# A shorter root, a sink as a score column, and gate products on the tensor engine, in an fp32 decoder layer

## The chip, the cores and the metric

The kernel runs on one core of a Trainium2 chip. The metric is the device time of one execution in microseconds. A core has five engines with a queue of instructions each: PE (TensorE, matrix products; its weight loads are shown apart as PEld), DVE (VectorE), ACT (ScalarE), POOL (GpSimd) and SP (SyncE, which here issues nearly all DMAs). Each engine works through its queue in order, and waits for another on semaphores.

## The reference

One layer of a hybrid decoder (Hymba-style): a sequence of 512, width 1024, 8 heads of 64 in group A (sliding window of 128, with a sink for each head), 8 in group B (native sparse attention with the branches cmp, sel and win, each with a sigmoid gate). Cut to what matters:

```
mod = silu(c) @ w_ada + b_ada;  shift, scale, gate = split(mod, 3)
h = rms_norm(x, norm_gain) * (1 + scale) + shift
q_a, k_a, v_a, z_a, q_b, kc, vc, ks, vs, kw, vw, z_b, g_b = split(h @ w_in)
qk_norm(t, gain) = t * rsqrt(mean(t * t) + EPS) * gain            # on every q and k
# group A, sliding window with a sink:
m = max(max(logits), sink);  e = exp(logits - m)
p = e / (sum(e) + exp(sink - m));  o_a = p @ v
# group B: o_cmp (31 compressed blocks), o_sel, o_win
gb = sigmoid(g_b + b_nsa_gate)
o_b = gb[0] * o_cmp + gb[1] * o_sel + gb[2] * o_win
y = concat(o_a * silu(z_a), o_b * silu(z_b))
out = x + gate * (y @ w_out)
```

## The kernel before

Everything is fp32. A large product is made of three fast ones: the weight is split into an upper and a lower half (`split`: `wh` is a copy by ACT, `wl` the difference `raw - wh`), the activations likewise (`hh`, `hl`), and each block of 128 in the contraction takes `wh·hh`, `wl·hh` and `wh·hl`. A weight matrix comes in four pieces p. `wl` is DVE's work for p = 0, 1, 2 (`WL_DVE`), and POOL's for p = 3.

The stages, with their places in the profiled execution: the start (modulation with `c`, sum of squares, normalised `h`), then the first projection (q, k, v of group A), to about 62 us; stream 1, which projects the compressed, selected and window keys and values and the q of group B, woven with 16 "a" slots of attention, to about 165; stream 2, which makes the z projections, the compressed attention and the gate, woven with 28 "b" slots, to about 310; the output projection in eight units, each with a DMA of its result.

A slot is one head pair's block of 128 queries in one branch. It runs in four steps, one iteration apart: scores (PE into PSUM, a custom DVE instruction that adds the bias and keeps the running minimum `nm`, Exp on ACT with its sum in `dn`), scale (DVE: `rr = 1/dn`, times P), transposes (PE, copied by ACT), and value products (PE). `run` takes the slots in turn and advances the stream by a budget for each, 3.6 in stream 1 and 1.5 in stream 2; a generator in the stream yields the cost of what it has just issued. The work that follows a projection (`posts`: norms, q and k scaling, `cmp_mlp`, the gate) is woven into the following units by `with_posts`. A scheduler then orders the instructions by their dependences; only the start has its order written out (`in_order`).

`rsqrt` is the root of the norms, on DVE: an integer guess and three Newton steps, twelve operations on tiles of 128x1 to 128x40, in 11 calls. Four of these belong to the q of group B (128x8): `post_q` squares (`sq`, L510), sums (`ss_q`, L514), scales (L517), takes the root (L100 to L109, ending in `n_y`), multiplies (`qn`, L523), splits (`qc`, L526 and L527), and PE transposes `qc` (L532).

In an "a" slot the sink is a small chain of its own: `es = nm + sink` (L880), its Exp (L886), `dn += es` (L901). In a "b" slot `rr` is multiplied by the head's gate (`grev`, L905, and L895 with L898 in the slot that holds two branches of the first block).

`gate_slice(q)` makes a quarter of the output gate's modulation on POOL: eight products of a weight block with a column of silu(c) (`gt`, L707, and L704 for the first), and seven sums into `gacc` (L708). At the output stage PE sums `gacc` over the partitions (L1008). The weights come through `rawp`, a ring of five buffers that also carries all other weights; `load_next` issues the next DMA on SP's queue.

One tile `longs` holds `gacc`, the values `va`, `vs`, `vw`, `kg`, `gsig`, `grev`, the ones, `nsink` and columns for the modulation; another, `hhl`, holds the 16 halves of `h` and an identity. In the profile their parts read as `longs` and `hhl`.

Of the kernel before, what the change touches and what calls it, by code (L numbers as in the profile page):

```python
# [77 lines left out]
def hybrid_layer_kernel(ctx, tc, A, out):  # L78
# [11 lines left out]
    def T2(dt, name):  # L90
        return t2.tile([128, S], dt, name=name, tag="t2")

    def rsqrt(v, n):
# [8 lines left out]
        DVE.tensor_scalar(hv, v, -0.5, None, op0=OP.mult)
        cur = yi.bitcast(F32)
        DVE.tensor_tensor(p, hv, cur, op=OP.mult)
        for n in range(3):
            DVE.tensor_tensor(t, p, cur, op=OP.mult)
            DVE.scalar_tensor_tensor(y, t, 1.5, cur, op0=OP.add, op1=OP.mult)
            if n < 2:
                DVE.scalar_tensor_tensor(p, t, 1.5, p, op0=OP.add, op1=OP.mult)  # L109
# [14 lines left out]
    hhl = con.tile([128, 16 * S + 128], F32R, name="hhl")  # L124
    hh, hl = ([hhl[:, S * (8 * e + k):S * (8 * e + k + 1)] for k in range(8)] for e in range(2))
    ident_r = hhl[:, 16 * S:16 * S + 128]
    longs = con.tile([128, 3040], F32, name="longs")
    used = [0]

    def keep(*shape):  # L130
        n = int(np.prod(shape))
        used[0] += n
        t = longs[:, used[0] - n:used[0]]
        return t if len(shape) == 1 else t.rearrange("p (a b) -> p a b", a=shape[0])

    gacc = keep(D)
    va, vs, vw = (keep(NB, 128) for _ in range(3))
    kg = keep(4, HD)
    gsig, grev = keep(NB, 24), keep(NB, 24)
    ones, nsink, sc_col, prm1 = keep(1), keep(8), keep(8), keep(8)  # L140
# [25 lines left out]
    def split(g, p):  # L166

        if g in COL:
            src = raws[g, p % 2][:, :, 128 * (p // 2):128 * (p // 2) + 128]
# [6 lines left out]
        ACT.activation(wh, src, AF.Copy)  # L176
        (DVE if p in WL_DVE else POOL).tensor_tensor(wl, src, wh.bitcast(F32), op=OP.subtract)  # L177
# [405 lines left out]
    def cmp_x(kv, bank):  # L583

        tt = T2(F32, "cmpt").rearrange("p (g u) -> p g u", g=2)
        for g in range(2):
            for par in range(2):
                src = bank[64 * g:64 * g + 64, par:512:2]
                dst = tt[64 * par:64 * par + 64, g, :]
                if g:  # L590
# [65 lines left out]

    def cmp_attn():
        kTc = X["kTc"]
        L = [mp.tile([128, 2, 2, 128], F32, name="pa", bufs=3) for _ in range(2)]
        for g in range(2):  # L660
            ps = ps_s.tile([128, 512], F32, name="s")
            for r in range(4):
# [34 lines left out]
            yield 0.44  # L697

    def gate_slice(q):
        g = gacc[:, 256 * q:256 * q + 256]  # L700
        for j in range(8):
            a = raws[f"gate{q}", j // 4][:, j % 4]
            if j == 0:
                POOL.tensor_scalar(g, a, sc_col[:, 0:1], None, op0=OP.mult)  # L704
            else:
                t = mp.tile([128, 256], F32, name="gt", bufs=4)
                POOL.tensor_scalar(t, a, sc_col[:, j:j + 1], None, op0=OP.mult)  # L707
                POOL.tensor_tensor(g, g, t, op=OP.add)  # L708
# [146 lines left out]
    def slot_scores(sl):  # L855
        kind, r, br, i = sl["id"]
        lo = max(0, i - 1) * 128 if kind == "a" else 0
        w = (i + 1) * 128 - lo
# [7 lines left out]
        for g in range(2):  # L866
# [9 lines left out]
            DVE.tensor_tensor_reduce(out=P[:, g, 0:w], in0=ps, in1=bt, scale=1.0, scalar=init,  # L876
                                     op0=OP.add, op1=OP.min, accum_out=nm[:, g:g + 1])
        if kind == "a":
            es = sm.tile([128, 2], F32, name="es", bufs=4)
            DVE.tensor_tensor(es, nm, sinks[:, r:8:4], op=OP.add)  # L880
# [4 lines left out]
        if kind == "a":
            ACT.activation(es, es, AF.Exp)  # L886
        sl.update(P=P, dn=dn, w=w, lo=lo)

    def slot_scale(sl):
        kind, r, br, i = sl["id"]  # L890
        P, dn, w = sl["P"], sl["dn"], sl["w"]
        if br == 3:
            rr = sm.tile([128, 2, 2], F32, name="rr2", bufs=2)
            DVE.reciprocal(rr, dn)
# [4 lines left out]
            return
        if kind == "a":  # L900
            DVE.tensor_tensor(dn, dn, sl["es"], op=OP.add)  # L901
        rr = sm.tile([128, 2], F32, name="rr", bufs=4)
        DVE.reciprocal(rr, dn)
        if kind == "b":
            DVE.tensor_tensor(rr, rr, grev.rearrange("p i (g r c) -> p i g r c", g=2, c=3)[:, i, :, r, br], op=OP.mult)  # L905
        for g in range(2):
            if kind == 'a' and g: ACT.activation(P[:, g, 0:w], P[:, g, 0:w], AF.Copy, scale=rr[:, g:g + 1])
            else: DVE.tensor_scalar(P[:, g, 0:w], P[:, g, 0:w], rr[:, g:g + 1], None, op0=OP.mult)
# [175 lines left out]
```

## Time and profile before

| | |
|---|---|
| median of 3 runs | 356.04 us (355.6 to 356.32) |
| profiled execution | 355.26 us, of which span 353.5 us |
| mean granted PE clock | 0.989 |
| busy: PE, DVE, ACT, POOL | 331.8, 248.9, 198.7, 70.7 us |
| DMA | 44.28 MB, mean 125 GB/s |

A row of the profile names a line of the kernel, an engine, an operation, and the tiles written and read (`out<-in`). Windows give the busy time of each engine in a stretch; a group's row has its busy time, the mean ns of one, and the idle time ahead of it with what ended that. A wait reads `PE pt L532 <- DVE qc L527`: PE's instruction at L532 was idle until DVE's at L527 ended; then come the total, the times and the longest.

### The profile page before, as it was taken

To read this page: it belongs to the slowest core of one execution; us is meant where nothing else is said; L and a number is where in the kernel's file an instruction comes from. 1 tells how busy PE (TensorE), PEld (TensorE's weight loads), DVE (VectorE), ACT (ScalarE), POOL (GpSimd) and SP (SyncE) were. 2 spreads that over 40 slices of the span, in tenths; PEclk is the share of its full clock that TensorE was granted. 3 is DMA by queue.
4 is the path that set the end of the run, shared out by engine and by line. 5 is a ranking of instruction groups with operands and counts; after the bars stand their busy time and mean duration, and the time that the engine had idled before them with its cause. 6 is when DMAs were issued, how large, how long until landed. Compare 5 with 4: busy or idle time off the path is not lost.

```text
span 353.5 us, 6376 instructions
## 1 busy us (share of the span) xinstructions
PE 331.8 (94%) x2239; PEld 262.2 (74%) x2240; DVE 248.9 (70%) x823; ACT 198.7 (56%) x510; POOL 70.7 (20%) x81
## 2 busy tenths in 40 slices
PE   8999999999799998697898899999999999999995
PEld 4478888788766797686855586788788788788884
DVE  3657797999886689996957699878767673643321
ACT  6665538367476585574754667867777666322200
POOL 1000001020200017646449007700100100110110
PEclk9999999999899999998999999999999999999999
DMA  8999926700155442233173035201101203124221
GB/s 266 390 410 406 376 96 161 259 0 3 61 170 194 144 124 86 92 119 121 31 209 121 0 111 162 85 4 59 61 2 47 75 4 117 59 62 118 73 76 59
DMA packets 31063, 44.28 MB, mean 125 GB/s; under 512 B 1766, under 2 KB 23398, under 8 KB 31032
## 3 DMA queue, kind: packets, MB, share of 16 engines
q1 hardware_dynamic: 29880, 41.79, 35.3%
q10 hardware_dynamic: 1152, 2.10, 2.1%
q8 instruction: 17, 0.28, 0.3%
q14 instruction: 14, 0.11, 0.1%
HBM read 41.74 MB, written 2.14 MB: 124 GB/s over the span
## 4 chain that ended last, share of the span: by engine, by line
PE 66%; DVE 16%; POOL 5%; DMA 5%; ACT 3%; issue 2%; SPq 1%; DVEq 0%; ACTq 0%; POOLq 0%
PE pj L494 23%; PE po L944 7%; PE s L871 6%; PE sq L301 5%; PE pj L484 5%; PE pt L926 3%; DMA raw<-in_w_gate 3%; POOL gt L707 3%; PE skv L327 2%; PE pt L919 2%; PE skv L302 2%; PE s L609 2%; POOL longs L708 2%; DVE wl L177 2%; DVE pp L600 1%
## 5 line engine op out<-in xcount | busy, mean ns | idle before, releaser
L177 POOL TENSOR_TENSOR wl<-raw,wh 128x512 fp32r<-128x512 f32 (+1 forms) x13 | 18.8, 1447 | 253.0 <-PE pj L494 100.3
L484 PE MATMUL pj<-wh,hhl 128*128 128x256 f32 (+1 forms) x256 | 55.1, 298 | 0.0
L494 PE MATMUL pj<-hhl,wh 128*128 128x512 f32 x160 | 52.1, 405 | 0.0
L176 ACT ACTIVATE wh<-raw 128x512 fp32r<-128x512 f32 (+1 forms) x52 | 31.6, 626 | 26.3 <-PE pj L494 25.3
L484 PEld LDWEIGHTS pj<-wh,hhl 128*128 128x128 f32 x256 | 42.1, 192 | 2.3 <-issue 2.2
L484 PE MATMUL pj<-wl,hhl 128*128 128x256 f32 (+1 forms) x128 | 37.8, 295 | 1.9 <-DVE wl L177 1.9
L177 DVE TENSOR_TENSOR wl<-raw,wh 128x512 fp32r<-128x512 f32 (+1 forms) x39 | 26.9, 697 | 17.5 <-PE pj L494 14.3
L883 ACT ACTIVATE pp<-pp,nm 128x256 f32<-128x256 f32 (+2 forms) x48 | 29.3, 612 | 16.4 <-DVE nm L876 15.8
L494 PEld LDWEIGHTS pj<-hhl,wh 128*128 128x128 f32 x160 | 28.1, 188 | 8.0 <-issue 3.8
L944 PE MATMUL po<-ptT,longs 128*64 128x128 f32 x432 | 33.7, 284 | 0.0
L876 DVE CUSTOM_DVE_ANT_0 pp<-s,bias 128x256 f32<-128x256 f32 (+2 forms) x48 | 25.3, 552 | 10.0 <-PE s L871 6.3
L494 PE MATMUL pj<-hhl,wl 128*128 128x512 f32 x80 | 31.8, 398 | 0.0
L944 PEld LDWEIGHTS po<-ptT,longs 128*64 128x64 f32 x432 | 24.1, 138 | 9.7 <-issue 4.6
L707 POOL TENSOR_SCALAR gt<-raw,longs 128x256 f32<-128x256 f32 x28 | 26.1, 940 | 4.3 <-DMA raw<-in_w_gate 4.3
L484 PEld LDWEIGHTS pj<-wl,hhl 128*128 128x128 f32 x128 | 24.7, 193 | 2.8 <-DVE wl L177 2.1
L871 PE MATMUL s<-kTb,qs 128*128 128x256 f32 (+2 forms) x96 | 24.7, 365 | 1.5 <-DVE nm L876 0.9
L494 PE MATMUL pj<-yh,wh 128*128 128x512 f32 x64 | 25.6, 401 | 0.0
L494 PE MATMUL pj<-yl,wh 128*128 128x512 f32 x64 | 25.2, 394 | 0.0
L494 PE MATMUL pj<-yh,wl 128*128 128x512 f32 x64 | 25.2, 393 | 0.0
L301 PE MATMUL sq<-swh,hhl 128*128 128x512 f32 x64 | 23.5, 404 | 0.3 <-ACT hhl L380 0.3
L883 ACT ACTIVATE pa<-pa,nm 128x256 f32<-128x256 f32 (+1 forms) x32 | 15.3, 478 | 11.5 <-DVE nm L876 11.4
L708 POOL TENSOR_TENSOR longs<-longs,gt 128x256 f32<-128x256 f32 x28 | 21.5, 766 | 0.6
(227 smaller groups left out, 716.6 us busy)
## 6 DMA issues: line engine op xcount, KB each, us to landing
ada_ring<-in_w_ada_ss SPq DMA_DIRECT2D x16, 512.0 KB, 7.4
raw<-in_w_cmp SPq DMA_DIRECT2D x8, 512.0 KB, 6.1
raw<-in_w_gate SPq DMA_DIRECT2D x8, 512.0 KB, 5.0
raw<-in_w_o SPq DMA_DIRECT2D x8, 512.0 KB, 3.8
wst_ring<-in_w_qkv_a SPq DMA_DIRECT2D x8, 384.0 KB, 8.1
xTp<-in_xT SPq DMA_DIRECT2D x8, 256.0 KB, 4.8
raw<-in_w_q_b SPq DMA_DIRECT2D x4, 512.0 KB, 5.2
bias<-line_d SPq DMA_DIRECT2D x8, 256.0 KB, 3.7
```

What stands on the lines that cost most here:

```text
L176: ACT.activation(wh, src, AF.Copy)
L177: (DVE if p in WL_DVE else POOL).tensor_tensor(wl, src, wh.bitcast(F32), op=OP.subtract)
L301: PE.matmul(pj_q[tb], lt, w[:, 0:512], start=f, stop=l, skip_group_check=True)
L484: PE.matmul(bank[:, t * n:(t + 1) * n], h[:, tb * 128:(tb + 1) * 128], w[:, k % 2, :], start=k == 0 and m == 0, stop=k == 7 and m == 2)
L494: PE.matmul(bank, w, h, start=k == 0 and m == 0, stop=k == 7 and m == 2)
L707: POOL.tensor_scalar(t, a, sc_col[:, j:j + 1], None, op0=OP.mult)
L708: POOL.tensor_tensor(g, g, t, op=OP.add)
L871: PE.matmul(ps, qs[h][:, 128 * i:128 * i + 128], k[:, hl_, lo:lo + w], start=hl_ == 0, stop=hl_ == 1)
L876: DVE.tensor_tensor_reduce(out=P[:, g, 0:w], in0=ps, in1=bt, scale=1.0, scalar=init, op0=OP.add, op1=OP.min, accum_out=nm[:, g:g + 1])
L883: ACT.activation(P[:, g, 0:w], P[:, g, 0:w], AF.Exp, bias=nm[:, g:g + 1], scale=-1.0, accum_out=dn[:, g:g + 1])
L926: PE.transpose(pt[:, b * 128:(b + 1) * 128], P[:, g, b * 128:(b + 1) * 128], ident)
L944: PE.matmul(o[64 * g:64 * g + 64, 128 * i:128 * i + 128], vb[:, 64 * g:64 * g + 64], sl["T"][:, g, b, :], start=first_of and b == 0, stop= ...
```

## The change

Seven edits at once:

1. `rsqrt` takes eight operations, with other constants and one integer operation for the guess.
2. The sink becomes one more column of an "a" slot's score tile (`pa`, now 2 x 257): POOL copies `nsink` into column w, the Exp runs over w + 1 columns and its sum includes the sink. `es` and its three operations go.
3. The gate factor of a "b" slot goes into the scale, as its second per-partition scalar; the slot with two branches scales in four pieces of 128.
4. `gate_slice` makes its products on PE: eight products of 32 columns (`scz`) by 256 into four row groups of a PSUM bank, and one ACT copy into `gacc`. It takes a bank of the projections, and yields 1.3 instead of 0.
5. `wl` for p = 3 goes from POOL to DVE.
6. The memset ahead of the compressed keys goes from POOL to DVE, ordered behind the start.
7. The parts of `longs` and `hhl` become tiles of their own (the halves of `h` come from the `t2` pool, which grows from 15 buffers to 31).

```diff
     def rsqrt(v, n):
-        yi = sm.tile([128, n], I32, name="n_yi")
...
-        for n in range(3):
-            DVE.tensor_tensor(t, p, cur, op=OP.mult)
-            DVE.scalar_tensor_tensor(y, t, 1.5, cur, op0=OP.add, op1=OP.mult)
-            if n < 2:
-                DVE.scalar_tensor_tensor(p, t, 1.5, p, op0=OP.add, op1=OP.mult)
-            cur = y
+        y = sm.tile([128, n], F32, name="n_y")
+        t = sm.tile([128, n], F32, name="n_t")
+        DVE.tensor_scalar(y.bitcast(I32), v.bitcast(I32), -0.5, float(MAGIC), op0=OP.mult, op1=OP.add)
+        DVE.tensor_tensor(t, y, y, op=OP.mult)
+        DVE.scalar_tensor_tensor(t, t, -0.375 * NEWTON[0], v, op0=OP.mult, op1=OP.mult)
+        DVE.scalar_tensor_tensor(y, t, 0.375 * NEWTON[0] * NEWTON[1], y, op0=OP.add, op1=OP.mult)
+        DVE.tensor_tensor(t, y, y, op=OP.mult)
+        DVE.scalar_tensor_tensor(t, t, 64.0 / 9.0, v, op0=OP.mult, op1=OP.mult)
+        DVE.scalar_tensor_tensor(t, t, -10.0 / 3.0, t, op0=OP.add, op1=OP.mult)
+        DVE.scalar_tensor_tensor(y, t, 5.0, y, op0=OP.add, op1=OP.mult)
         return y
...
-        (DVE if p in WL_DVE else POOL).tensor_tensor(wl, src, wh.bitcast(F32), op=OP.subtract)
+        DVE.tensor_tensor(wl, src, wh.bitcast(F32), op=OP.subtract)
...
     def gate_slice(q):
-        g = gacc[:, 256 * q:256 * q + 256]
-        for j in range(8):
...
+        pm = PJ()[:, 0:256]
+        for h in range(2):
+            for c in range(4):
+                PE.matmul(pm[32 * c:32 * c + 32, :], scz[:, 4 * h + c, :], raws[f"gate{q}", h][:, c], start=h == 0,
+                          stop=h == 1, skip_group_check=True)
+            load_next()
+        ACT.activation(gacc[:, 256 * q:256 * q + 256], pm, AF.Copy)
+        yield 1.3
...
+        e = w
         if kind == "a":
-            es = sm.tile([128, 2], F32, name="es", bufs=4)
-            DVE.tensor_tensor(es, nm, sinks[:, r:8:4], op=OP.add)
-            sl["es"] = es
+            POOL.tensor_copy(P[:, :, w:w + 1], nsink[:, r:8:4][:, :, None])
+            e = w + 1
         for g in range(2):
-            ACT.activation(P[:, g, 0:w], P[:, g, 0:w], AF.Exp, bias=nm[:, g:g + 1], scale=-1.0,
+            ACT.activation(P[:, g, 0:e], P[:, g, 0:e], AF.Exp, bias=nm[:, g:g + 1], scale=-1.0,
                            accum_out=dn[:, g:g + 1])
-        if kind == "a":
-            ACT.activation(es, es, AF.Exp)
...
     def slot_scale(sl):
...
-        if kind == "b":
-            DVE.tensor_tensor(rr, rr, grev.rearrange("p i (g r c) -> p i g r c", g=2, c=3)[:, i, :, r, br], op=OP.mult)
...
+            if kind == "b":
+                DVE.tensor_scalar(v, v, rr[:, g:g + 1], gates[:, g, br:br + 1], op0=OP.mult, op1=OP.mult)
```

How this moves instructions, at three places. First POOL's queue from the second slice of the gate on, before:

```order
L177 TENSOR_TENSOR wl<-raw,wh 128x512 [waits DMAHW0_49,PE_49,Activation_49]
L704 TENSOR_SCALAR longs<-raw,longs 128x256 [waits DMAHW1_49]
L707 TENSOR_SCALAR gt<-raw,longs 128x256 x2
L708 TENSOR_TENSOR longs<-longs,gt 128x256 [waits Pool_49]
L707 TENSOR_SCALAR gt<-raw,longs 128x256 [waits DVE_49]
L708 TENSOR_TENSOR longs<-longs,gt 128x256 [waits Pool_49] x2
L707 TENSOR_SCALAR gt<-raw,longs 128x256 [waits DMAHW2_49]
```

and all that POOL does after its first memset now:

```order
L869 COPY pa<-nsink 128x2 [waits DMAHW4_49,DMAHW5_49,DMAHW2_49,DMAHW7_49,DVE_49,Activation_49]
L869 COPY pa<-nsink 128x2 [waits DVE_49,PE_49]
L869 COPY pa<-nsink 128x2
L869 COPY pa<-nsink 128x2 [waits DVE_49,PE_49,Pool_49]
L869 COPY pa<-nsink 128x2 [waits PE_49,DVE_49,Activation_49,Pool_49] x12
```

POOL's queue goes from 73 rows to 14: the gate's products and sums and the lower halves are gone from it, and sixteen copies of two elements have come.

Second PE's queue at the first sel or win slots of the second b head (`s` are scores, `pt` transposes, `po` value products, and `pj<-hhl,wh` z projections), before:

```order
L871 MATMUL s<-kTb_732,qs_1960 128x256 [waits Activation_49]
L871 MATMUL s<-kTb_732,qs_1960 128x256
L871 MATMUL s<-kTb_734,qs_2272 128x256
L944 MATMUL po<-ptT,longs 64x128 [waits PE_49,Activation_49]
L944 MATMUL po<-ptT,longs 64x128 x3
L871 MATMUL s<-kTb_734,qs_2272 128x256
L494 MATMUL pj<-hhl,wh 128x512 x2
L494 MATMUL pj<-hhl,wl 128x512
```

and now:

```order
L860 MATMUL s<-kTb_751,qs_1895 128x256 [waits DVE_49,PE_49]
L860 MATMUL s<-kTb_751,qs_1895 128x256
L933 MATMUL po<-ptT,vw 64x128
L696 MATMUL pj<-raw,scz 32x256 [waits DMAHW2_49]
L696 MATMUL pj<-raw,scz 32x256
L933 MATMUL po<-ptT,vw 64x128 [waits Activation_49]
L915 MATMUL pt<-first,pp 128x128 [waits DVE_49,PE_49]
L915 MATMUL pt<-first,pp 128x128 x3
L933 MATMUL po<-ptT,vw 64x128 [waits Activation_49]
L933 MATMUL po<-ptT,vw 64x128 x3
```

The gate's products (L696, which wait for the DMAs of their weights) stand in PE's queue among the attention rows, and the z projections that stood there have moved behind.

Third DVE's queue in a root of the q of group B (`n_t`, `n_y`, `n_p`), woven with a slot's scores, before:

```order
L106 TENSOR_TENSOR n_t<-n_p,n_yi 128x8 [waits DVE_49]
L880 TENSOR_TENSOR es<-nm,rest 128x2 [waits DVE_49]
L107 SCALAR_TENSOR_TENSOR n_y<-n_t,n_yi 128x8 [waits DVE_49]
L109 SCALAR_TENSOR_TENSOR n_p<-n_t,n_p 128x8
L565 CAST kTb_734<-pt 64x2x256 [waits Activation_49]
L106 TENSOR_TENSOR n_t<-n_p,n_y 128x8 [waits DVE_49]
L901 TENSOR_TENSOR dn<-dn,es 128x2 [waits Activation_49]
L876 ISA pa,nm<-s,bias,longs 128x128 [waits DMAHW1_49,PE_49]
```

and now the whole root of one call:

```order
L96 TENSOR_SCALAR n_y<-ss_q 128x8 [waits DVE_49]
L97 TENSOR_TENSOR n_t<-n_y 128x8 [waits DVE_49]
L865 ISA pa,nm<-s,bias,nsink 128x256 [waits PE_49,Pool_49]
L865 ISA nm 128x1
L98 SCALAR_TENSOR_TENSOR n_t<-n_t,ss_q 128x8 [waits DVE_49]
L99 SCALAR_TENSOR_TENSOR n_y<-n_t,n_y 128x8 [waits DVE_49]
L100 TENSOR_TENSOR n_t<-n_y 128x8 [waits DVE_49]
L865 ISA pa,nm<-s,bias,nsink 128x256 [waits PE_49]
L865 ISA nm 128x1
L101 SCALAR_TENSOR_TENSOR n_t<-n_t,ss_q 128x8 [waits DVE_49]
L102 SCALAR_TENSOR_TENSOR n_t<-n_t 128x8 [waits DVE_49]
L103 SCALAR_TENSOR_TENSOR n_y<-n_t,n_y 128x8 [waits DVE_49]
```

The `es` and `dn` rows of the sink are gone from DVE, and the root's rows are fewer.

More of the change, by code (lines that the diff above doesn't have):

```diff
@@ L22 @@
 BIG = 1e30
-MAGIC = 0x5F3759DF
+MAGIC, NEWTON = 0x5F1FFFF9, (0.703952253, 2.38924456)
 BUCKET_STARTS = [0, 1, 2, 3, 4, 5, 6, 7, 8, 9, 10, 11, 12, 13, 14, 15, 16, 19, 21, 24, 27, 31, 35, 40,
@@ L63, in in_order @@
 @contextmanager
-def in_order(tc):
+def in_order(tc, after=()):
     traced = tc.nc.cur_bb.bb.instructions
     n = len(traced)
-    yield
+    last = dict(after)
+    yield last
     info = mybir.DependencyInfo(mybir.DependencyClass.NoSync, mybir.DependencyReason.DATA)
-    last = {}
     for i in tc.nc.cur_bb.bb.instructions[n:]:
@@ L122, in hybrid_layer_kernel @@
     bnsa, sinks = sml[:, 384:408], sml[:, 408:416]
[L124 to L140, printed above, removed]
+    ident_r = con.tile([128, 128], F32R, name="ident_r")
+    ones = con.tile([128, 1], F32, name="ones")
     DVE.memset(ones, 1.0)
+    hh = [T2(F32R, f"hh{k}") for k in range(8)]
+    hl = [T2(F32R, f"hl{k}") for k in range(8)]
+    gacc = con.tile([128, D], F32, name="gacc")
     line_d = dram.tile([2, 8, LINE], F32, name="line_d")
+    kg = con.tile([128, 4, HD], F32, name="kg")
+    nsink = con.tile([128, 8], F32, name="nsink")
+    sc_col = con.tile([128, 8], F32, name="sc_col")
+    prm1 = con.tile([128, 8], F32, name="prm1")
+    va = con.tile([128, NB, 128], F32, name="va")
+    vs = con.tile([128, NB, 128], F32, name="vs")
+    vw = con.tile([128, NB, 128], F32, name="vw")
+    gsig = con.tile([128, NB, 24], F32, name="gsig")
+    grev = con.tile([128, NB, 24], F32, name="grev")
     raw_order = [(g, h) for g in ("kv_cmp", "kv_sel", "kv_win_g") for h in range(2)]
@@ L303, in first_proj @@
                       skip_group_check=True)
-    with in_order(tc):
+    with in_order(tc) as begun:
         zero = con.tile([128, 512], BF16, name="zero")
@@ L594, in cmp_x @@
         x = mp.tile([128, 16, 2, 32], F32, name="pp", bufs=3)
-        POOL.memset(x[:, :, :, 31:32], 0.0)
+        with in_order(tc, begun):
+            DVE.memset(x[:, :, :, 31:32], 0.0)
         base = tt[:, :, 0:1]
@@ L658, in cmp_attn @@
         kTc = X["kTc"]
-        L = [mp.tile([128, 2, 2, 128], F32, name="pa", bufs=3) for _ in range(2)]
+        L = [mp.tile([128, 2, 257], F32, name="pa", bufs=3).rearrange("p a b -> p (a b)")[:, 0:512]
+             .rearrange("p (a b c) -> p a b c", a=2, b=2) for _ in range(2)]
         for g in range(2):
@@ L858, in slot_scores @@
         w = (i + 1) * 128 - lo
-        P = mp.tile([128, 2, 256], F32, name="pa", bufs=3) if kind == "a" else mp.tile([128, 2, 512], F32, name="pp", bufs=3)
+        P = mp.tile([128, 2, 257], F32, name="pa", bufs=3) if kind == "a" else mp.tile([128, 2, 512], F32, name="pp", bufs=3)
         if br == 3:
@@ L891, in slot_scale @@
         P, dn, w = sl["P"], sl["dn"], sl["w"]
+        gates = grev.rearrange("p i (g r c) -> p i g r c", g=2, c=3)[:, i, :, r]
         if br == 3:
@@ L894, in slot_scale @@
             DVE.reciprocal(rr, dn)
-            DVE.tensor_tensor(rr, rr, grev.rearrange("p i (g r c) -> p i g r c", g=2, c=3)[:, 0, :, r, 1:3], op=OP.mult)
-            Pv = P[:, :, 0:256].rearrange("p g (b k) -> p g b k", b=2)
             for g in range(2):
-                DVE.tensor_tensor(Pv[:, g], Pv[:, g], rr[:, g, :, None].to_broadcast([128, 2, 128]), op=OP.mult)
+                for b in range(2):
+                    v = P[:, g, 128 * b:128 * b + 128]
+                    DVE.tensor_scalar(v, v, rr[:, g, b:b + 1], gates[:, g, 1 + b:2 + b], op0=OP.mult, op1=OP.mult)
             return
-        if kind == "a":
-            DVE.tensor_tensor(dn, dn, sl["es"], op=OP.add)
         rr = sm.tile([128, 2], F32, name="rr", bufs=4)
         DVE.reciprocal(rr, dn)
-        if kind == "b":
-            DVE.tensor_tensor(rr, rr, grev.rearrange("p i (g r c) -> p i g r c", g=2, c=3)[:, i, :, r, br], op=OP.mult)
         for g in range(2):
-            if kind == 'a' and g: ACT.activation(P[:, g, 0:w], P[:, g, 0:w], AF.Copy, scale=rr[:, g:g + 1])
-            else: DVE.tensor_scalar(P[:, g, 0:w], P[:, g, 0:w], rr[:, g:g + 1], None, op0=OP.mult)
+            v = P[:, g, 0:w]
+            if kind == "b":
+                DVE.tensor_scalar(v, v, rr[:, g:g + 1], gates[:, g, br:br + 1], op0=OP.mult, op1=OP.mult)
+            elif g:
+                ACT.activation(v, v, AF.Copy, scale=rr[:, g:g + 1])
+            else:
+                DVE.tensor_scalar(v, v, rr[:, g:g + 1], None, op0=OP.mult)
     def slot_trans(sl):
```

21 lines of the change are left out of this document (1 added, 20 removed).

## The prediction

> **What bounds the kernel now.** I read the page first: busy times, the slices, the chain that ended last.
>
> ```profile
> PE 331.8 (94%) x2239; PEld 262.2 (74%) x2240; DVE 248.9 (70%) x823; ACT 198.7 (56%) x510; POOL 70.7 (20%) x81
> ...
> PE   8999999999799998697898899999999999999995
> ...
> POOL 1000001020200017646449007700100100110110
> ...
> PE 66%; DVE 16%; POOL 5%; DMA 5%; ACT 3%; issue 2%; SPq 1%; DVEq 0%; ACTq 0%; POOLq 0%
> ```
>
> PE is idle for 353.5 − 331.8 = 21.7 us in all; that is the most a change off PE can gain. Its weak slices lie where POOL's row is dense. The windows, cut by stage, put numbers on it (columns: length, then busy time of PE, PEld, DVE, ACT, POOL; then the granted clock).
>
> ```profile
> 62.00:82.00 20.00, 18.82 (x124) 16.29 (x122) 19.16 (x53) 11.30 (x30) 1.97 (x1) 1.00 0.32 112
> 82.00:100.00 18.00, 15.71 (x117) 14.08 (x115) 16.28 (x60) 10.64 (x39) 2.01 (x1) 0.91 0.11 33
> 100.00:136.00 36.00, 35.71 (x281) 28.14 (x277) 27.41 (x135) 25.03 (x78) 2.62 (x3) 1.00 0.55 175
> 136.00:200.00 64.00, 52.21 (x391) 41.51 (x389) 50.28 (x191) 35.92 (x102) 38.78 (x46) 0.97 0.32 96
> 200.00:255.00 55.00, 54.12 (x384) 41.49 (x381) 46.89 (x150) 38.50 (x103) 15.74 (x17) 1.00 0.25 77
> 255.00:308.00 53.00, 53.00 (x399) 42.76 (x398) 32.36 (x108) 33.60 (x85) 2.58 (x2) 1.00 0.15 47
> ```
>
> From 136 to 200 PE idles 64.00 − 52.21 = 11.8 us, and POOL works 38.8 of the 64; from 200 to 255 it idles 0.9, from 100 to 136 0.3, from 62 to 100 (1.2 + 2.3) 3.5 us. So the middle holds more than half of all PE idleness. Which wait ends last there: the list of waits, for PE and for those who wait for POOL.
>
> ```profile
> PE pt L532 <- DVE qc L527: 5.3, 3, 2.3
> PE s L871 <- DVE nm L876: 4.0, 3, 2.6
> PE pt L560 <- ACT kc L554: 2.6, 2, 1.9
> PE pj L484 <- DVE wl L177: 1.9, 1, 1.9
> ...
> POOL longs L704 <- DMA raw<-in_w_gate: 11.1, 4, 4.8
> POOL gt L707 <- DMA raw<-in_w_gate: 4.3, 2, 2.8
> DVE pp L876 <- POOL longs L708: 3.7, 1, 3.7
> ACT oa L954 <- POOL longs L708: 1.8, 1, 1.8
> ACT cst L666 <- POOL longs L708: 1.8, 1, 1.8
> DVE qn L523 <- POOL longs L708: 1.6, 1, 1.6
> ```
>
> PE never waits for POOL directly, but for DVE and ACT, and these stood behind POOL's gate products (L704 to L708). The chain of waits, asked for 138 to 200 alone, shows the hand-over; its summary by line, and six pieces:
>
> ```profile
> by line: DMA raw<-in_w_gate 15.1%; POOL gt L707 14.6%; POOL longs L708 10.9%; issue 4.3%; DVE n_t L106 4.2%; PE po L944 3.6%; DVE pa L876 3.0%; POOL longs L704 3.0%; PE pj L484 3.0%; PE s L871 2.8%; ACT wh L176 2.5%; DVE n_p L109 2.4%; DVE
> ...
> 159.70 0.90 POOL gt L707
> 160.60 0.71 POOL longs L708
> ...
> 161.34 0.69 DVE qn L523
> ...
> 162.13 0.63 ACT qc L526
> ...
> 162.78 0.70 DVE qc L527
> ...
> 163.62 0.51 PE pt L532 x4
> ```
>
> 15.1 + 14.6 + 10.9 + 3.0 = 43.6% of that stretch is gate loads and gate products, though no q, score or transpose uses a gate before the output stage. POOL has a second effect, seen in the timeline of DVE: the same small operation beside POOL's products and just after them.
>
> ```profile
> 146.68 0.69 DVE L109 SCALAR_TENSOR_TENSOR n_p<-n_t,n_p 128x8 f32<-128x8 f32 x1
> 148.76 0.16 DVE L109 SCALAR_TENSOR_TENSOR n_p<-n_t,n_p 128x8 f32<-128x8 f32 x1
> ```
>
> **The change, part by part.** The rows that price it:
>
> ```profile
> L177 DVE TENSOR_TENSOR wl<-raw,wh 128x512 fp32r<-128x512 f32 x36 | 24.7, 694 | 17.5 <-PE pj L494 14.3 <-issue 3.0
> 18.69 1.07 PE L234 MATMUL pj<-ada_ring,scz 128*32 128x256 f32 x16
> L238 ACT ACTIVATE macc<-pj 128x256 f32<-128x256 f32 x5 | 1.9, 384 | 2.4 <-PE pj L234 2.4
> L109 DVE SCALAR_TENSOR_TENSOR n_p<-n_t,n_p 128x4 f32<-128x4 f32 (+3 forms) x22 | 4.8, 217 | 0.0
> L901 DVE TENSOR_TENSOR dn<-dn,es 128x2 f32<-128x2 f32 x16 | 3.3, 203 | 1.1 <-ACT es L886 1.1
> L880 DVE TENSOR_TENSOR es<-nm,rest 128x2 f32<-128x2 f32 x16 | 2.5, 155 | 0.1
> L905 DVE TENSOR_TENSOR rr<-rr,longs 128x2 f32<-128x2 f32 x24 | 5.7, 236 | 0.6
> ```
>
> *Gate products on PE: +4.3 us.* Today's modulation (L234) is the same shape: 8 products, 16 instructions, against 32 columns of `scz`, 1.07 us. Four slices cost 4 × 1.07 = 4.3 us of PE. The ends are 0 (if they fall into idle PE time) and 4.3; PE is 94% busy and I give idle time away below, so I take the whole. The four ACT copies add 4 × 0.38 = 1.5 us to an engine that is busy 36 of 64 in the middle: nothing on the path, with ACT slack 28 us as its cover. A rule that speaks against this part is in the Trainium skill, "TensorEngine Tiling (Array Packing)", section Key Properties: changing the tiling mode drains the array. By the order the four slices stand in seven pieces, so fourteen changes; if each cost one value product's 0.08 us (L944 below), an estimate, the sum would be 1.1 us worse, −3.3 in place of −4.4. The trace does not bear that out: 255 to 308 alternates 64-column products (`po`) with full ones and has PE at 53.00 busy of 53.00.
>
> *What the gate leaves behind on POOL: −12.7 + 4.5 us of PE idleness.* The order shows POOL with sixteen two-element copies and no gate and no `wl`. Nothing on DVE or ACT then stands behind a gate sum, and raw buffers are freed by PE rather than by POOL. The idle time at stake is 11.8 + 0.9 = 12.7 us (136 to 255). What stays is bounded below by the neighbouring stage: 200 to 255 has DVE at 46.9 of 55 and idles 0.9, so about 1.0. It is raised by a new place. The order of PE shows that from the second branch of the first b head to the second branch of the next one only 4 `z` products are left between the attention rows, where sixteen stood before, since the gates now use up the stream's budget (4 × 1.3 of it) and the `z` units slide behind. Counted in the order, this stretch holds 26 score, 40 transpose and 32 value products, the gates and those 4. Their prices, as busy time over count (PE's products overlap, so the mean of one is longer):
>
> ```profile
> L944 PE MATMUL po<-ptT,longs 128*64 128x128 f32 x432 | 33.7, 284 | 0.0
> L871 PE MATMUL s<-kTb,qs 128*128 128x256 f32 (+2 forms) x96 | 24.7, 365 | 1.5 <-DVE nm L876 0.9
> L926 PE MATMUL pt<-first,pp 128*128 128x128 f32 x112 | 15.2, 275 | 0.2 <-DVE pp L908 0.2
> L494 PE MATMUL pj<-hhl,wh 128*128 128x512 f32 x160 | 52.1, 405 | 0.0
> ```
>
> 26 × 24.7/96 + 40 × 15.2/112 + 32 × 33.7/432 + 4 × 0.4 + 4.3 = 6.7 + 5.4 + 2.5 + 1.6 + 4.3 = 20 us of PE. DVE and ACT have in 200 to 308 together 46.9 + 32.4 = 79 and 38.5 + 33.6 = 72 us; by the order that time holds 152 of the transposes, so 40/152 of it falls on the stretch, 21 and 19, less what the change takes from DVE. Three engines near 90% in one chain: PE will wait. Ends: nothing, and 20/0.75 − 20 = 6.7 us (52 of 64 busy in the middle today is 0.82; 0.75 is the worst I allow). I take 3.5, near the middle. Left over: 1.0 + 3.5 = 4.5.
>
> *Root in eight operations instead of twelve (the ninth is the scaling ahead of it).* 11 calls. In the middle stand the four q calls; each has 4 operations fewer at 0.217, and the other 8 back from 0.217 to 0.16 once POOL is silent, about 1.3 us each, 5 of DVE. This lies on the path to `qc` (5.3 us of waits), and is how the idle time above goes; it is no term of its own. At the start the chain of the first root ends while PE is still on the modulation: nothing.
>
> *Sink as a column.* DVE loses 16 × (0.155 + 0.203) = 5.7 us, ACT its 16 small Exp; a third of that lies after 136. POOL's copy waits only for its `pa` buffer, three slots ahead of the Exp, so it is hidden; if that cover were gone, an Exp would start later by one small POOL operation (no row; at most the 0.71 us of a 256-column sum in the chain above). The row of 257 has no price here: ends 0 and one two-hundred-and-fifty-sixth of an Exp.
>
> *Gate factor in the scale.* DVE loses 24 × 0.236 = 5.7 us, all after 164, where PE mostly does not wait for DVE: cover for the bare stretch, else nothing. Two pointer scalars instead of one in the scale have no row; the nearest, one pointer, is the scale itself; ends 0 and +0.1 us each, off the path outside the stretch.
>
> *Lower halves (`wl`) all on DVE.* 13 more pieces at 0.69: 9 us, of it by POOL's old order three in the middle, 2.1. DVE there: 50.3 − 5 − 2 + 2.1 = 45 in a stage that shrinks to about 57: below the 85% at which 200 to 255 hardly idles. At 82 to 100 DVE is at 16.3 of 18; there `wl` adds about 1.4 and the roots give about as much back: 0, ends −1.5 and +1.5, and the 1.9 us wait for `wl` stays.
>
> *Memset, buffers apart.* One DVE memset; separate tiles free waits that only shared names made. The stage 255 to 308 has no idle PE, so nothing there.
>
> *Clock.* The granted clock is 0.91 in 82 to 100 and 0.97 in 136 to 200, 1.6 + 1.9 us' worth, at most. With shorter stalls some returns: −0.5, ends 0 and −1.5. (The Trainium skill, "TensorE: Matmul & The Clock Gate", section What's actually happening, has the clock halve after an idle window of 3.4 us; the trace's stalls are 2.6 us at most and the clock still dropped, so I do not count on its return.)
>
> **Sum.** +4.3 − 12.7 + 4.5 + 0 − 0.5 = −4.4 us. The profiled execution took 355.26 (span 353.5 and 1.76 around it), so 350.9; it lies 0.78 below the median of the runs, which gives 356.04 − 4.4 = 351.6.
>
> **Rivals.**
> *The waits stay.* PE's late inputs come from DVE's in-order queue, not from POOL, or the bare stretch takes its upper price. For: the PE rows name DVE, not POOL; against: the 43.6% above. Then −12.7 + 1.0 + 6.7 + 4.3 = −0.7: 355.3.
> *PE inherits the gate loads: slower.* POOL stood 11.1 + 4.3 us for `in_w_gate` and nobody else stopped; in PE's in-order queue the same wait stops everything. Two waits of 4.8 give +9.6 − 4.4 = +5.2: 361. It decides from 4.4 us of such waits. Against: with the products on PE a raw buffer is freed after half a slice, about 0.5 us, instead of after four POOL products and their sums (0.9 and 0.7 each in the chain), so the next load starts earlier, and the longest of POOL's waits, 4.8, began with a load issued late.
> *More than that.* The bare stretch has no stall, the clock comes back and 62 to 100 gains 1: −12.7 + 1.0 + 4.3 − 1.5 − 1 = −9.9: 346.1.
>
> **Chances.** Forecast 0.55, waits stay 0.17, gate loads 0.13, more 0.15. Faster by over 0.2% (about what a measurement of this kernel can tell): nearly all of the forecast, the last rival and half of the first, 0.77; same 0.06; slower 0.17. Range 347 to 357: it leaves out the far end of the biggest gain and most of the gate-load case.
>
> **What would show it.** POOL's busy time under 10 us; L696 products of 1.0 to 1.1 us a slice with no DMA wait in PE's list; the waits `pt <- qc` gone or under 1 us; PE busy about 336, with idleness of 12 to 14 us of which the largest new piece lies between the two b heads; DVE's busy time near 232. I am wrong if PE waits for `in_w_gate`, or if `qc` and `nm` keep their places in the list with POOL silent.

## The result, and the profile after

| | before | after |
|---|---|---|
| median of 4 runs | 356.0 us (355.6 to 356.32) | 346.95 us (346.34 to 347.62) |
| profiled execution, its span | 355.26, 353.5 us | 347.51, 345.6 us |
| PE busy, PE idle in the span | 331.8, 21.7 us | 337.1, 8.5 us |
| granted PE clock in that execution | 0.989 | 0.995 |

The ratio is 0.9747, with a 95% interval of 0.9721 to 0.9773: faster by 9.05 us, where 4.4 were forecast and 347 was the lower end of the range. Of the page, the rows that were shown of before:

```profile
PE 337.1 (98%) x2304; PEld 263.5 (76%) x2304; DVE 236.9 (69%) x742; ACT 199.6 (58%) x499; POOL 4.9 (1%) x22
...
PE   8999999998999999999999999999999999999995
...
POOL 1000000000000000000000000000000000000000
...
PE 88%; DVE 6%; ACT 2%; DMA 1%; issue 1%; SPq 0%; DVEq 0%; ACTq 0%
```

POOL has left the chain, and so have the DMAs of the gate. The windows, with the columns as before:

```profile
62.00:82.00 20.00, 18.72 (x121) 16.20 (x120) 18.89 (x51) 11.66 (x32) 0.31 (x2) 1.00 0.01 4
82.00:100.00 18.00, 17.35 (x118) 14.69 (x118) 16.12 (x54) 10.85 (x35) 0.19 (x1) 0.91 0.10 31
100.00:136.00 36.00, 35.68 (x282) 28.51 (x282) 26.31 (x111) 23.23 (x68) 1.84 (x7) 1.00 0.53 161
136.00:200.00 64.00, 63.29 (x478) 50.46 (x478) 52.27 (x190) 43.12 (x117) 0.94 (x5) 1.00 0.25 75
200.00:255.00 55.00, 55.00 (x437) 40.39 (x436) 39.18 (x132) 39.94 (x111) 0.00 (x0) 1.00 0.33 106
```

From 136 to 255 PE idles 0.7 us instead of 12.7. DVE is busier there than before (52.3 of 64, against 50.3) and hardly holds PE up any more. The granted clock came back from 0.97 to 1.00 from 136 to 200, and stayed at 0.91 from 82 to 100. What is left in the list of PE's waits, and the chain of 138 to 200 by line, which was 43.6% gate before:

```profile
PE skv L317 <- DVE wst_ring L299: 1.2, 1, 1.2
PE pt L522 <- DVE qs L531: 1.2, 2, 0.7
PE pj L474 <- DVE wl L167: 0.6, 1, 0.6
PE s L860 <- DVE nm L865: 0.5, 1, 0.5
...
by line: PE pj L474 24.6%; PE pj L484 17.2%; PE s L860 12.9%; PE po L933 10.6%; PE s L655 6.7%; PE pt L908 6.5%; PE pt L522 5.2%; PE pt L915 2.7%; PE pj L696 1.6%; ACT kTb L554 1.4%; PE pt L686 1.4%; PE pt L662 1.4%; ACT ptT L909 1.4%; DVE 
```

The gate's products stand in seven pieces, that is, runs of instructions with other products between them. Their group, and four of the pieces from PE's timeline (start, length, instructions at the end):

```profile
L696 PE MATMUL pj<-raw,scz 128*32 128x256 f32 x64 | 5.3, 389 | 0.0
...
192.74 1.07 PE L696 MATMUL pj<-raw,scz 128*32 128x256 f32 x16
203.75 0.63 PE L696 MATMUL pj<-raw,scz 128*32 128x256 f32 x4
207.03 1.06 PE L696 MATMUL pj<-raw,scz 128*32 128x256 f32 x12
211.76 0.64 PE L696 MATMUL pj<-raw,scz 128*32 128x256 f32 x8
```

### The profile page after: what moved, and what is told of

Same layout as the page of the kernel before. It is cut to its first block, busy times and chain, and to the rows that moved or that the text cites. A ratio compares the mean times of both kernels' runs of the same rounds, so it can differ in the third digit from the quotient of the medians.

```text
span 345.6 us, 6354 instructions
## 1 busy us (share of the span) xinstructions
PE 337.1 (98%) x2304; PEld 263.5 (76%) x2304; DVE 236.9 (69%) x742; ACT 199.6 (58%) x499; POOL 4.9 (1%) x22
## 4 chain that ended last, share of the span: by engine, by line
PE 88%; DVE 6%; ACT 2%; DMA 1%; issue 1%; SPq 0%; DVEq 0%; ACTq 0%
PE pj L484 28%; PE pj L474 11%; PE po L933 9%; PE s L860 8%; PE sq L291 7%; PE pt L915 4%; PE skv L292 3%; PE pt L908 3%; PE s L600 3%; PE pj L224 1%; PE po L939 1%; PE pj L696 1%; PE pt L522 1%; DMA xTp<-in_xT 1%; PE s L655 1%; DVE wl L167 1%
## 5 line engine op out<-in xcount | busy, mean ns | idle before, releaser
L474 PE MATMUL pj<-wl,hh 128*128 128x256 f32 (+1 forms) x128 | 37.7, 295 | 0.6 <-DVE wl L167 0.6
L474 PE MATMUL pj<-wh,hh 128*128 128x256 f32 (+1 forms) x128 | 38.0, 297 | 0.1
L474 PE MATMUL pj<-wh,hl 128*128 128x256 f32 (+1 forms) x128 | 37.6, 294 | 0.0
L484 PE MATMUL pj<-hh,wh 128*128 128x512 f32 x80 | 33.1, 413 | 0.0
L484 PE MATMUL pj<-hh,wl 128*128 128x512 f32 x80 | 31.8, 397 | 0.0
L484 PE MATMUL pj<-hl,wh 128*128 128x512 f32 x80 | 31.7, 396 | 0.0
L474 PEld LDWEIGHTS pj<-wh,hh 128*128 128x128 f32 x128 | 24.6, 192 | 1.7 <-issue 1.5
L474 PEld LDWEIGHTS pj<-wl,hh 128*128 128x128 f32 x128 | 24.7, 193 | 1.6 <-DVE wl L167 0.8
L474 PEld LDWEIGHTS pj<-wh,hl 128*128 128x128 f32 x128 | 24.6, 193 | 0.4 <-issue 0.3
L893 DVE TENSOR_SCALAR pp<-pp,rr,grev 128x256 f32<-128x256 f32 (+2 forms) x48 | 21.6, 476 | 0.6
```

The source lines that it names most:

```text
L474: PE.matmul(bank[:, t * n:(t + 1) * n], h[:, tb * 128:(tb + 1) * 128], w[:, k % 2, :], start=k == 0 and m == 0, stop=k == 7 and m == 2)
L484: PE.matmul(bank, w, h, start=k == 0 and m == 0, stop=k == 7 and m == 2)
L893: DVE.tensor_scalar(v, v, rr[:, g:g + 1], gates[:, g, br:br + 1], op0=OP.mult, op1=OP.mult)
```

## The experiments

Idleness is the span less PE's busy time, in the profiled execution; it is the measure that tells the theories apart, since PE's busy time also varies with the clock and with how narrow products fall in its queue. Ratios are to the kernel before, run on the same chip.

| run | median us | ratio (95% interval) | PE busy | idle | clock |
|---|---|---|---|---|---|
| after | 346.95 | 0.9747 (0.9721 to 0.9773) | 337.1 | 8.5 | 0.995 |
| e1 gate on PE alone | 347.1 | 0.9765 (0.9704 to 0.9826) | 336.3 | 10.0 | 0.993 |
| e2 no gate | 341.41 | 0.9606 (0.9546 to 0.9666) | 328.2 | 10.3 | 1.000 |
| e3 root alone | 358.66 | 1.0084 (1.005 to 1.0118) | 334.5 | 21.5 | 0.981 |
| e4 shared tiles | 346.82 | 0.9757 (0.9704 to 0.981) | 337.4 | 7.7 | 1.000 |
| e5 POOL busy beside | 360.6 | 1.0147 (1.0125 to 1.0168) | 341.6 | 16.1 | 0.995 |
| e6 barer stretch | 348.77 | 0.9822 (0.9806 to 0.9838) | 338.2 | 8.5 | 1.000 |
| e7 gate on DVE | 343.11 | 0.9666 (0.9642 to 0.9691) | 331.2 | 9.5 | 0.998 |
| e8 rest without the gate | 345.9 | 0.9734 (0.9687 to 0.9781) | 332.2 | 11.7 | 0.995 |
| e9 private product tile | 349.2 | 0.9836 (0.9802 to 0.987) | 332.2 | 15.3 | 0.990 |
| e10 e5, private tile | 352.29 | 0.9924 (0.9894 to 0.9953) | 339.9 | 11.0 | 1.000 |
| e11 lower halves alone | 353.3 | 0.9962 (0.9939 to 0.9985) | 333.1 | 18.3 | 0.995 |
| e12 lower halves on POOL | 347.28 | 0.9788 (0.9739 to 0.9836) | 336.2 | 9.2 | 1.000 |
| e13 e9 and the root | 344.89 | 0.9696 (0.9652 to 0.974) | 328.7 | 15.0 | 1.000 |
| e14 e8, private tile | 343.35 | 0.9654 (0.9616 to 0.9692) | 329.6 | 11.8 | 1.000 |
| e15 gate on DVE alone | 345.42 | 0.9711 (0.967 to 0.9753) | 332.6 | 11.3 | 0.995 |
| e16 e9 and the lower halves | 345.51 | 0.9742 (0.9687 to 0.9796) | 330.7 | 12.7 | 0.999 |

**e1, e2: the gate alone.** In the kernel before, e1 replaces `gate_slice` by the changed one; e2 replaces POOL's work by a copy, so that its output lacks the gate factor:

```diff
-                POOL.tensor_scalar(t, a, sc_col[:, j:j + 1], None, op0=OP.mult)
-                POOL.tensor_tensor(g, g, t, op=OP.add)
+            if j % 4 == 0:
+                ACT.activation(g, a, AF.Copy)
```

> The kernel before with one part of the change: the gate products on PE, nothing else. Theory P (POOL's gate made nearly all the idleness of the middle): PE busy +5.3, idleness of PE between 136 and 255 from 12.7 to 3 us or less, time 350 +- 1.5. Rival D (DVE's own load made it; root, sink and factor are what helped): idleness falls by 3 us at most, time 356 to 359. Rival B (shared tiles tie unrelated work together): as D.

> The kernel before with the gate products left out: an ACT copy of one weight block stands for four products and sums, so the output's gate factor is not computed; its loads and the release of their buffers stay. Theory P: idleness of the middle gone without the PE cost, 345 to 347. Rival D: 353 to 356. If e1 minus e2 is 4 to 5.5 us, the gate's PE time is paid in full; if it is under 2, PE takes it in idle time.

e1 is as fast as the whole change, within the intervals. Both times lie below what theory P gave (347.1 against 350 ± 1.5, 341.41 against 345 to 347). Its window of the middle (first row) has no idleness worth the name, with DVE's load untouched by root, sink and factor:

```profile
136.00:200.00 64.00, 63.15 (x483) 49.69 (x479) 53.91 (x226) 43.68 (x124) 2.65 (x2) 1.00 0.24 74
```

So DVE at 53.9 of 64 was not the bound, and rival D falls; so does B, since e1 keeps the shared tiles. e2 is 5.7 us below e1 in the medians, with about the same idleness (10.3 and 10.0): PE pays for the gate's 5.3 us of products in full.

**e3, e4: root alone, tiles shared again.**

```diff
-        for n in range(3):                                      # e3, in the kernel before
...
+        DVE.tensor_tensor(t, y, y, op=OP.mult)
...
-    gacc = con.tile([128, D], F32, name="gacc")                 # e4, in the changed kernel
...
+    hhl = con.tile([128, 16 * S + 128], F32R, name="hhl")
+    longs = con.tile([128, 3040], F32, name="longs")
```

> The kernel before with the root of eight operations alone. Theory P: POOL still holds qn, nm and oa back, gain 0 to 2 us, 354 to 356. Rival D: the path to qc gets 1.3 us shorter four times, gain 4 to 6 us, 350 to 352.

> The changed kernel with the parts of longs and hhl in shared tiles again, as before (t2 15 buffers). Theories P and D: with POOL quiet the shared names tie nothing that matters, 347 +- 0.7. Rival B: idleness of PE comes back by 3 us or more, 350 or above.

The shared names cost nothing (346.82). The shorter root alone makes the kernel slower by 0.8%, which no theory had. DVE's busy time falls (242.8 us, from 248.9), but PE's idleness stays (21.5, from 21.7), and waits for POOL grow (the longest before were 3.7, 1.8, 1.8 and 1.6). What is longer is PE's busy time, 334.5 against 331.8, at a granted clock of 0.981 against 0.989; why is open.

```profile
ACT oa L948 <- POOL longs L702: 4.1, 2, 2.2
ACT zth L785 <- POOL longs L702: 3.1, 1, 3.1
ACT sq L504 <- POOL longs L702: 2.8, 1, 2.8
DVE pa L870 <- POOL longs L702: 2.6, 2, 2.3
ACT cst L660 <- POOL longs L702: 2.3, 1, 2.3
```

None of these instructions reads a product of the gate. In the built program of the kernel before, the output tiles of such waits (`qn`, `sq`, `pp`, `cst`, `oa`) lie at addresses where a product tile `gt` lay: the allocation hands the memory of each freed tile on, and the next owner must wait until POOL has read it. Whether this is what costs time was tried in e9.

**e5, e10: POOL kept busy beside.** e1 with all lower halves on DVE, and with 60 operations of the gate's shapes on POOL:

```diff
+        for j in range(15):
+            t = mp.tile([128, 256], F32, name="gt", bufs=2)     # e10: one tile, kept for good
+            if j % 2:
+                POOL.tensor_tensor(t, d[:, 0:256], d[:, 256:512], op=OP.add)
+            else:
+                POOL.tensor_scalar(t, d[:, 0:256], sc_col[:, 0:1], None, op0=OP.mult)
```

> e1 with all lower halves on DVE, and with POOL given 60 operations of the gate's shapes on tiles of its own, for which nobody waits (they read finished q and key tiles; the output is the reference's). It keeps POOL as busy as before and takes the waits away. Theory W (others waited for POOL's sums, and for buffers that it held): DVE gets slower beside POOL, but PE hardly idles, 347 to 349.5. Rival C (the slowing of DVE beside POOL made the idleness): PE idles 8 us or more again, 354 to 358.

e5 did not do what it says. Its tiles came out of the shared memory too, and others did wait for them:

```profile
ACT ptT L924 <- POOL gt L713: 3.0, 1, 3.0
DVE pp L851 <- POOL gt L713: 2.8, 1, 2.8
ACT cst L666 <- POOL gt L713: 2.6, 1, 2.6
```

As a test of contention it is void; by accident it shows that products which nobody uses slow the kernel through their memory alone: 16.1 us of idleness against 11.0 in e10, which differs by the private tile only.

> e5 again with POOL's 60 operations writing one tile of their own, since e5's tiles were taken from shared memory and ACT and DVE waited for them (3.0, 2.8, 2.6 and 1.9 us). Gate products on PE, all lower halves on DVE. Theory M: 347 to 350, as e1. Rival C: 354 or above.

e10's time fell between the two. Its idleness is only 1.0 us above e1's, with POOL at 55.5 us of work; the rest of the loss is PE's busy time, 3.6 us, of which the gate's products are 2.7. They stand in twelve pieces there:

```profile
L705 PE MATMUL pj<-raw,scz 128*32 128x256 f32 x64 | 8.0, 390 | 0.0
...
201.19 0.62 PE L705 MATMUL pj<-raw,scz 128*32 128x256 f32 x2
201.74 0.73 PE L876 MATMUL s<-kTb,qs 128*128 128x512 f32 x2
```

After a piece of two instructions the next product starts only 0.55 us later. The nearer neighbour is the changed kernel, which like e10 has all lower halves on DVE: against its 8.5 us e10 idles 2.5 us more. So POOL's work beside the others is worth 1.0 to 2.5 us of idleness here, and rival C is not the main cause; the expectation had not thought of the order.

**e6: a barer stretch.**

```diff
-        yield 1.3
+        yield 4.0
```

> The changed kernel with a cost of 4.0 instead of 1.3 yielded for each gate slice, so that still more z work slides behind the attention slots. Theory S (the bare stretch would stall as the prediction had it, and 1.3 is just short of it): PE idles 5 us or more in the b slots, 351 to 354. Rival N (DVE and ACT keep up without the z products): 347 +- 1.

Nothing stalls: the idleness is 8.5 us as in the changed kernel, and 200 to 255 is full.

```profile
200.00:255.00 55.00, 55.00 (x460) 40.24 (x460) 40.20 (x153) 43.48 (x126) 0.00 (x0) 1.00 0.28 87
```

It is 0.0075 slower in the ratio, above the changed kernel's interval and outside rival N's 347 ± 1; its PE is busy 1.1 us longer, though the gate's products take 5.3 us there too. Why was not followed up.

**e8, e11, e12: the rest, and the lower halves.** e8 is the changed kernel with POOL's gate, the sink's chain and the shared tiles of before; e11 and e12 move one line:

```diff
-        (DVE if p in WL_DVE else POOL).tensor_tensor(wl, src, wh.bitcast(F32), op=OP.subtract)
+        DVE.tensor_tensor(wl, src, wh.bitcast(F32), op=OP.subtract)      # e11 in the kernel before; e12 the reverse in the changed one
```

> The changed kernel with the gate on POOL, the sink's own chain and the shared tiles of before: root, factor, lower halves on DVE and the memset are all that is left of the change. Theory P: nothing is gained, 355 to 358. Rival D: 350 to 353.

> The kernel before with all lower halves on DVE and nothing else. In e8 (root, factor, lower halves, memset) no instruction was held by POOL for long although the gate ran there. If it was the lower halves that kept POOL's gate late: 346 to 349. If it was how the build happened to lay out the memory there: 353 to 357, with waits for POOL in the list.

> The changed kernel with the lower halves of p = 3 on POOL again; POOL's sixteen sink copies then stand in a queue with them. If DVE's 9 us matter: 345.5 to 346.5. If nothing but PE's own work bounds the kernel: 347 +- 1. If an Exp waits for a sink copy behind a lower half: 348 to 351.

e8 is the surprise: without the gate's move it has the whole gain. POOL works 33.9 us from 136 to 200 there,

```profile
136.00:200.00 64.00, 59.55 (x430) 47.74 (x430) 56.16 (x186) 39.84 (x109) 33.91 (x40) 0.97 0.28 89
```

yet its list of waits has nobody waiting for a gate operation. The parts of the change replace each other; they do not add up. In e8's built program memory of the gate's products is handed on too, but not to the `sq` and `qn` that waited in the kernel before; that this is why nobody waits is not shown. e11 alone takes 3.4 us of the idleness away, and still has waits of 3.5 and 2.8 us for the gate's sums, as its second reading (the layout of the memory) had it. e12 shows that without a gate on POOL the lower halves may stay there.

**e9, e16: two holds.** The kernel before, with POOL's gate as it was:

```diff
+    gts = [con.tile([128, 256], F32, name=f"gt{n}") for n in range(1)]
...
-                t = mp.tile([128, 256], F32, name="gt", bufs=4)
+                t = gts[j % 1]
```

> The kernel before with one edit: the gate's products stand in one tile of their own (128x256, kept for good) instead of four from the shared memory, whose addresses the build hands on to qn, sq, pp, cst, oa and others. POOL does all its work as before; DVE, ACT and PE have no wait for a gate operation left. Theory M (memory handed on by the slow gate made the idleness): PE idles 4 us or less between 136 and 200, time 344 to 348. Rival C (DVE slowed beside POOL): 352 to 357. Rival Q (the gate's late loads and raw buffers): 352 to 357.

The idleness falls by 6.4 us, from 136 to 200 from 11.8 to 6.0. No engine's list names a gate operation any more, with POOL as busy there as before (40.3 against 38.8):

```profile
136.00:200.00 64.00, 58.03 (x430) 46.24 (x427) 56.21 (x207) 39.69 (x110) 40.33 (x47) 0.97 0.29 91
```

So handed-on memory did hold DVE and ACT; the shared tile `longs` is still there, and nobody waits through it. But theory M asked for 4 us or less from 136 to 200 and for 344 to 348, and e9 has 6.0 and 349.2: memory is a part of the cause. PE's longest waits there are for DVE still:

```profile
PE s L872 <- DVE nm L877: 2.4, 2, 2.1
PE pt L533 <- DVE qc L528: 2.3, 2, 1.2
```

> e9 (gate on POOL, products in a tile of their own) with all lower halves on DVE. PE's idleness in the whole span is the measure: 21.7 us before, 18.3 with the lower halves alone moved (e11), 15.3 in e9. Theory A (two separate holds, handed-on memory 6.4 and lower halves queued on POOL behind the gate 3.4, that add up): idleness 12 +- 1, as in e14 (11.8), time 344.5 to 347 by the clock that the runs get. Rival O (the two are one hold): idleness 14.5 or more, 348 or above.

e16 has e9's edit and e11's. Both give 12.7, inside what theory A said: 21.7 − 6.4 − 3.4 = 11.9 if they added up exactly. Its picture of lower halves queued on POOL behind the gate does not hold, however. In the kernel before, each lower half on POOL began after POOL had been idle, waiting for ACT or PE (the bracket), as these two after the second and third slices of the gate:

```profile
176.26 1.30 POOL L177 TENSOR_TENSOR wl<-raw,wh 128x512 fp32r<-128x512 f32 x1 [4.83 <-ACT qs L543]
211.20 1.53 POOL L177 TENSOR_TENSOR wl<-raw,wh 128x512 fp32r<-128x512 f32 x1 [16.05 <-PE pj L494]
```

And 1.5 us of what e11 takes away lies between 62 and 100 (idleness 3.5 to 2.0), before the gate begins. How the lower halves cost the rest is open. So is what remains from 136 to 200 with the gate on POOL: 6.0 us in e9 and 4.6 in e16, against 0.9 in e1. e10, with POOL busy 33.9 us there, idles 2.4, so work beside POOL can be a part of it; late loads and raw buffers were not tried alone.

Two small edits give the time of the whole change (345.51 and 346.95, intervals overlapping), with POOL still making the gate.

**e13, e14: does root or memory remain?**

> e9 (gate on POOL, products in a tile of their own) with the root of eight operations. PE still idles 6.0 us between 136 and 200 in e9, waiting for DVE, which is busy 56 of 64 there beside POOL. Theory C2 (with the handed-on memory gone, DVE's load beside POOL is what is left): now the shorter root helps, 345 to 348, though alone it made the kernel slower. Rival Q (late gate loads and raw buffers are left): 349 +- 1.

> e8 (root, factor, lower halves and memset, gate on POOL) with the gate's products in a tile of their own. By the trace e8 has hardly a wait for POOL left, so the private tile should add nothing: 345 to 347 (theory M: memory is the cause only where the build hands it on). If waits that the profile doesn't show were left in e8: 342 to 344.

e13's time (344.89, a hair below theory C2's 345 to 348) would speak for C2, but its cause is another. Its idleness is 15.0 against e9's 15.3; what fell is PE's busy time, 332.2 to 328.7, with the clock at 1.000 in the place of 0.990. The root bought next to no idleness. e14 has e8's idleness (11.8, 11.7): the private tile adds nothing where no wait was left; its 2.6 us less is busy time again (329.6, 332.2). By that measure theory M holds, though the time lies below its 345 to 347, where the other reading had it.

**e7, e15: the gate on DVE.**

```diff
+                DVE.scalar_tensor_tensor(g, a, sc_col[:, j:j + 1], g, op0=OP.mult, op1=OP.add)
```

> The changed kernel with the gate products on DVE: 32 operations of 128x256, two inputs, about 0.45 us each, 14.4 us of DVE, none on PE. If PE's 5.3 us for the gate are paid in full (e1 minus e2 was 5.7) and DVE has room (39 of 55 busy from 200 to 255): 341.5 to 343.5. If DVE's queue makes PE wait as POOL's did: 346 to 352.

> The kernel before with the gate on DVE as in e7, and nothing else of the change. DVE had 53.9 of 64 busy in the middle in e1 and gets 14 us more. If root, sink and factor buy nothing as long as DVE is off the path, this is where they should: 345 to 349, against 343.1 in e7. If DVE still has room: 342 to 344.

e7 beats both kernels: 343.11, PE busy 331.2 and DVE 245.6:

```profile
PE 331.2 (97%) x2240; PEld 261.0 (77%) x2240; DVE 245.6 (72%) x774; ACT 198.3 (58%) x494; POOL 4.5 (1%) x22
```

e15, without the rest of the change, is at 345.42 with 1.8 us more idleness: the intervals overlap (0.967 to 0.9753, 0.9642 to 0.9691), so the rest is worth about two microseconds there, if anything. e14, which leaves the gate on POOL, is as fast as e7.

## Why the prediction was wrong

The sign, the place and the resource were right: POOL's gate held DVE and ACT, these held PE in the middle, and of the 12.7 us of idleness from 136 to 255 all but 0.7 went. The time came out a hair below the range, with twice the gain. By the steps:

*Idleness that stays: 4.5 us forecast, 0.7 measured.* This is the term that failed, and within it the bare stretch (3.5). It makes 3.8 of the 4.65 us between forecast and result. The stretch without `z` products runs from 198 to 218 in the changed kernel:

```profile
198.00:218.00 20.00, 20.00 (x163) 13.09 (x162) 14.08 (x52) 15.85 (x45) 0.00 (x0) 1.00 0.63 212
```

PE's 20 us came out, though with other parts: half of the gate's products (3.0 us) and 60 value products in place of 32, so that agreement is partly luck. DVE and ACT were put at 21 and 19 by the share of transposes, and are 14 and 16. The windows they were scaled from hold the work of the z units too, which this stretch lacks: from 200 to 308 in the kernel before, the lower halves alone take DVE 8.29 us and the upper halves ACT 10.00, and the stretch has neither. The premise "three engines near 90%" was never there, and e6 shows that even more z work can leave without a wait. The forecast should have gone with its own bound from 255 to 308, where DVE at 61% left PE no idleness.

*Gate products: +4.3 forecast, 5.3 measured, paid in full.* The size is off by the pieces: 16 in a row take 1.07, but 4 to 8 take 0.63 to 0.64, so slices cut in two cost 1.28 to 1.69. The prediction weighed the Trainium skill's rule of "TensorEngine Tiling (Array Packing)", Key Properties, that a change of tiling mode drains the array, put 1.1 us on it, and set it aside. The trace has 1.0 us more than the uncut price, as that estimate had; e10 pays 3.7. The reason for setting it aside, a stage with PE busy 53.00 of 53.00, could not show it, since the short pieces here count as busy for all of their 0.63 us. Whether it is the drain or the latency of a short piece is not told apart.

*Clock: −0.5 forecast.* From 136 to 200 the clock came back in full, which the prediction put at 1.9 us; in the profiled pair it is not told apart from the rest, since PE's busy time rose by the 5.3 us of the gate and no less. Between runs there is an estimate: the four of the changed kernel are 346.34 and 346.40 at 1.000, 347.51 and 347.62 at 0.995, 1.2 us for 0.005. The runs of the kernel before beside the experiments stand at 0.978 to 0.990. From 0.985 to 0.9975 that makes about 3 us of the 9.05, which the profiled pair (0.989, 0.995) shows in part only: 7.75 us between those two executions. It is no firm price: e11 has 353.19 at 0.995 and 352.42 at 0.989.

*62 to 100: 0 forecast, −1.6 measured* (idleness 3.5 to 1.9). The stated end was −1.5, and "the 1.9 us wait for `wl` stays" failed: it is 0.6. e11 shows that the lower halves alone bring 1.5 us of this.

*Buffers and names.* "Separate tiles free waits that only shared names made": e4 refutes it with the gate on PE, e9 with the gate on POOL. *The root "is how the idle time goes"*: e1 refutes it, e3 leaves the idleness as it was, e13 finds next to none in it. *How POOL held the others* was not explained: the prediction named raw buffers and small operations slower beside POOL, where the waits of `qn` and its like were memory handed on (e9).

*The rivals.* "More than that", 346.1, is what came, with no stall in the stretch, a better clock, and 1.6 us for 1 from 62 to 100. PE did not wait for `in_w_gate` at all. Of the signs, POOL's 4.9 us and the vanished wait of `pt` for `qc` came; idleness of 12 to 14 us did not (8.5), and DVE is at 236.9, not near 232.

## What to carry to other kernels

When an instruction waits for an engine whose data it does not read, look at what lay in its output's memory before: in a kernel whose buffers are handed on, a slow engine's scratch tile is everybody's wait, and one private tile of 1 KB a partition took away 6.4 us of 21.7. Work given to the bound engine is paid there: with the gate on DVE (e7) or in private memory on POOL (e14) the kernel is 3.5 us faster than with it on PE. Test a bundle both by one part alone and by all but one, since parts that lift the same hold replace each other; and judge by the idleness of the bound engine, since a median can move by the clock. A stretch's load on the other engines is to be counted from its own instructions, not scaled from a window with other work in it.

## What was not expected of the hardware

Narrow products between full-width ones are priced by the piece: 2, 4, 6 or 8 instructions of 128x32 by 256 take 0.62 to 0.64 us, 12 to 16 take 1.06 to 1.07, so the same 64 cost 5.3 us in seven pieces and 8.0 in twelve.

The clock is lower where idleness is spread over short stalls: no kernel with under 13 us of idleness ran below 0.993 in its profiled execution, and the three at 0.990 or below have 15.3, 21.5 and 21.7 us, with no wait of PE over 3.2. It is no rule for a single one (e11, with 18.3, ran at 0.995, and e13, with 15.0, at 1.000), and which is cause and which effect no run shows.

POOL beside DVE cost little: with 55.5 us of POOL's work e10 idles 1.0 us more than e1 and 2.5 more than the changed kernel. The Trainium skill, "SBUF — State Buffer", section Who interferes with whom, has a DVE instruction with two SBUF inputs contend with a GpSimd instruction that reads SBUF. Single rows agree (0.69 against 0.16 us for `n_p`), but with DVE off the path little of it reaches the time.
